# A hybrid encoder block: constants on another queue, and half of attention's q and k turned by VectorE instead of TensorE

## The chip, the cores and the metric

The kernel runs on one core of a Trainium2 chip. Its time is the device time of one execution in microseconds; lower is better. The engines are TensorE (PE; its weight loads are PEld), VectorE (DVE), ScalarE (ACT), GpSimd (POOL) and SyncE (SP). SyncE only issues DMAs here; GpSimd issues DMAs and clears a few buffers.

## The reference

One layer of a block over 512 tokens (8 rows x 64 columns) of width 1024, in float32:

```python
x = x + FFN_RES * _swiglu(_rmsnorm(x, norm_ffn1), w_ffn1_gu, w_ffn1_down)      # d_ff 2816, FFN_RES 0.5
h = _rmsnorm(x, norm_mix)
xr, gr, q, k, v, ga, gb = jnp.split(h @ w_in, splits, axis=-1)                 # 7 x 1024 columns
xc = _centred_dwconv(xr, conv_w, conv_b)                                       # width 4
h_fwd = _rglru_scan(xc, ...); h_bwd = reversed scan                            # gated linear recurrences
y_lru = (h_fwd + h_bwd) * jax.nn.gelu(gr)
q = _rmsnorm(q per head, q_norm) * HEAD_DIM ** -0.5                            # 16 heads of 64
k = _rmsnorm(k per head, k_norm)
y_att = _neighbourhood_attention(q, k, v, rel_pos_bias)                        # window 8 rows x 16 columns
y = jax.nn.sigmoid(ga) * y_lru + jax.nn.sigmoid(gb) * y_att
x = x + y @ w_out
x = x + FFN_RES * _swiglu(_rmsnorm(x, norm_ffn2), w_ffn2_gu, w_ffn2_down)
```

## The kernel before

**Precision.** Each large product is made of three fast matmuls. An operand is split into a high part (a cast to float32r, by ScalarE or VectorE) and a low part (the rest, by a VectorE subtraction), and TensorE adds high·high, low·high and high·low in PSUM (names `xh`, `xl` for activations, `wh`, `wl` for weights). `split` (line 136) makes both; `load_w` (line 153) loads 512 KB of weights and splits them, with three raw buffers and four of each part, so weights are cast two or three chunks ahead of their use.

**Order.** A scheduler places the instructions on each engine by what is ready and by priority, not strictly in the order of the program; `after` and `hold` (lines 239 and 245) tie an instruction behind another one, `hold` behind the matmul that was written last. Buffers come from pools by tag: `big` has 42 tiles of 128 x 512, `pair` four of 1024 columns, `PT` five, `pt` two. There are four PSUM tiles of a kind called `acc` and four called `aux`.

**First stage** (`ffn` with `lead`, lines 469 to 494). For each of eight tiles k of x, SyncE loads x and a weight tile (the first weight tile on ScalarE's queue), ScalarE casts xh, casts the weights, squares x and scales it, VectorE makes the low parts, and TensorE runs 12 matmuls: for each of four token blocks xh·wh, xl·wh, xh·wl. xh needs the norm's scale, a column of `small`, a table of 114 constants per partition that GpSimd's queue loads (line 725). Eight matmuls on a tile of ones run ahead of this (line 131). Then the first feed-forward layer goes on in `strassen` (line 291).

**Middle stages.** `xr` projection and convolution, the recurrences (`lru`, line 799), then for each half hf of the heads q, k and v (`qk_raw`, `v_get`), then the gate projections (`gates`, line 1162: 24 chunks of 24 matmuls), then the output projection and the second feed-forward layer. Side work lies in "lanes": generators that `weave` advances at given rates while the projections go on (rates per stage in `RATE`). Attention is the lane `att`; the rest of v's layout is `v`, the recurrences are `lru`.

**Attention of a half** (`heads`, line 986). q and k come as tokens x features (four tiles each, `raws`). They are scaled by the norm (line 999); then for each fi of four pairs of heads `start(fi)` turns a 128 x 128 block per token group with TensorE, four for q (line 1008) and four for k (line 1010), into two aux tiles, and splits them into qh, ql, kh, kl, with the norm's gain `gq8` or `gk` (lines 1014 to 1019). `scores` (line 1023) runs the score matmuls (line 1040), VectorE adds the bias table `bm` and takes the maximum (line 1060), ScalarE does the exponential (line 1067), VectorE divides by the sum (line 1072). `ship` turns p by 32 x 32 blocks on VectorE, writes it to DRAM on SyncE's queue and fetches it turned on GpSimd's (line 1088, tile `PT`); `apply` multiplies by v (line 1103), for the second half two units later. `bias(g)` asks for the next table after the scores. `hT<-hd` and `PT<-pd` already use this way of turning: VectorE by blocks, and a DMA round trip through DRAM for the order of the blocks.

Of the kernel before, what the change touches and what calls it, by code (L numbers as in the profile page):

```python
# [9 lines left out]
F32 = mybir.dt.float32  # L10
# [70 lines left out]
    "t1": {"att": 0.75, "tail": 0.75, "lru": 2},  # L81
    "g": {"att": 0.7, "tail": 0.7, "lru": 1.5, "v": 0.5},
# [4 lines left out]
def block_kernel(ctx: ExitStack, tc, a, out):  # L87
# [19 lines left out]
    NBIG = 42  # L107
# [72 lines left out]
    def make_xg(gcol, tag):  # L180
# [6 lines left out]
        def one(k):  # L187
            g = small[:, gcol + k : gcol + k + 1]
            x = xres[k]
            mark["xh"] = nc.scalar.activation(xh[k], x, AF.Copy, scale=g)  # L190
            return nc.vector.scalar_tensor_tensor(xl[k], x, g, xh[k].bitcast(F32), ALU.mult, ALU.subtract)
# [269 lines left out]
    def ffn(wgu, ws, wd, xh, xl, forms, ssum, plain, res, emit_out, lead=None, end=None):  # L461
# [7 lines left out]
        if lead is not None:  # L469
            pre = [aux_t() for _ in range(NCB)]  # L470
            for k in range(KT):
# [6 lines left out]
                if k == 0:  # L478
                    cast = nc.vector.tensor_copy(H, raw)
                    after(lead[1](k), cast)  # L480
# [5 lines left out]
                for tb in range(NCB):  # L486
                    s = slice(tb * P, (tb + 1) * P)
                    nc.tensor.matmul(pre[tb], xh[k][:, s], H, start=k == 0, stop=False)
                    nc.tensor.matmul(pre[tb], xl[k][:, s], H, start=False, stop=False)  # L489
                    mark["mm"] = nc.tensor.matmul(pre[tb], xh[k][:, s], L, start=False, stop=k == KT - 1)  # L490
# [165 lines left out]
    lanes = {"att": [], "tail": [], "lru": [], "v": []}  # L656
    due = {"att": 0.0, "tail": 0.0, "lru": 0.0, "v": 0.0}
# [113 lines left out]
    gk = small[:, C_KN : C_KN + 1]  # L771
# [27 lines left out]
    def lru():  # L799
# [128 lines left out]
    def qk_raw(w, hf, st):  # L928
# [6 lines left out]
        for j, t in enumerate(raws):  # L935
            sq = big_t(n="sq")
# [49 lines left out]
    def heads(hf, raws, st):  # L986
# [9 lines left out]
        for w in range(2):  # L996
            for j in range(NCB):
                t = raws[w][j].rearrange("p (h d) -> p h d", d=HD)
                hold(nc.vector.tensor_tensor(t, t, rq[:, w, j, :].unsqueeze(2).to_broadcast([P, 8, HD]), ALU.mult))
            yield  # L1000
        qk, rss, soft, PTs = {}, {}, {}, {}


        def start(fi):
            fs = slice(fi * P, (fi + 1) * P)
            pq, pk = aux_t(), aux_t()
            for j in range(NCB):
                hold(nc.tensor.transpose(pq[:, j * P : (j + 1) * P], raws[0][j][:, fs], ident))
            for j in range(NCB):
                hold(nc.tensor.transpose(perm(pk)[:, j], raws[1][j][:, fs], ident))  # L1010
            rev = lambda t: t.rearrange("p (j t) -> p j t", j=NCB)[:, :, ::-1]
            fwd = lambda t: t.rearrange("p (j t) -> p j t", j=NCB)
            qh, ql, kh, kl = (big_t(F32R, n=n) for n in ("qh", "ql", "kh", "kl"))
            nc.scalar.activation(rev(qh), fwd(pq), AF.Copy, scale=gq8)
            with tc.high_priority():
                nc.vector.scalar_tensor_tensor(rev(ql), fwd(pq), gq8, rev(qh.bitcast(F32)), ALU.mult, ALU.subtract)
            nc.scalar.activation(kh, pk, AF.Copy, scale=gk)
            with tc.high_priority():
                mark["kl"] = nc.vector.scalar_tensor_tensor(kl, pk, gk, kh.bitcast(F32), ALU.mult, ALU.subtract)
# [3 lines left out]
        def scores(fi, n2s):  # L1023
# [22 lines left out]
            for n2, hp in [(n2, hp) for n2 in n2s for hp in range(2)]:  # L1046
# [78 lines left out]
        for i, (fi, n2s) in enumerate(units):  # L1125
            behind = scores(fi, n2s)
# [4 lines left out]
            if 0 in n2s:  # L1131
                if fi < 3:
                    start(fi + 1)
                if hf * 4 + fi + 1 < KT:
                    bias(hf * 4 + fi + 1)
# [18 lines left out]
    for hf in range(2):  # L1154
        st = tiny.tile([P, 2, NCB, 8], F32, tag="st", name=nm("st"))
        raws = [qk_raw(0, hf, st), qk_raw(1, hf, st)]
        v_get(hf)
        lanes["att"].append(heads(hf, raws, st))
# [148 lines left out]
```

## Time and profile before

| | us |
|---|---|
| three runs | 1086.52, 1087.53 (median), 1088.55 |
| profiled execution | 1086.78 |
| its span | 1085.0 |
| TensorE busy / weight loads | 1077.1 / 884.3 |
| VectorE busy | 770.1 |
| ScalarE busy | 561.9 |
| GpSimd busy | 198.6 |

The profile is of one execution; the span is from its first to its last instruction. In its rows, a line such as L1008 is a line of the kernel, "out<-in" names the tiles written and read, "x4" counts instructions. A row of the timeline has start, duration, engine, line, operation, tiles and, in brackets, how long the engine had been idle and what ended that. A row of the chain has start, time and the work that held the chain there. A row of the waits has the total, the number and the longest. Matmul durations overlap in the timeline, so their pitch is read from the chain.

### The profile page before, as it was taken

How to read it: one execution, taken by the hardware profiler on the slowest of the kernel's cores; microseconds unless marked ns; L12 is line 12 of the kernel's file. 1: busy time of each engine (PE TensorE's matmuls, PEld its weight loads, DVE VectorE, ACT ScalarE, POOL GpSimd, SP SyncE). 2: the span in 40 equal slices, each digit the busy share in tenths (PEclk: the TensorE clock that was granted, in tenths of full speed). 3: DMA queues.
4: the chain of work that ended last, by engine and by line, in shares of the span. 5: the costliest groups of instructions: out<-in, count | busy, mean ns of one | idle time of the engine just before them, and what ended most of it. 6: DMA issues, size and time to landing. Idle time of an engine off the chain costs nothing.

```text
span 1085.0 us, 14411 instructions
## 1 busy us (share of the span) xinstructions
PE 1077.1 (99%) x5121; PEld 884.3 (82%) x5121; DVE 770.1 (71%) x1222; ACT 561.9 (52%) x866; POOL 198.6 (18%) x341
## 2 busy tenths in 40 slices
PE   8999999999999999999999999999999999999998
PEld 7888888888888778788877888888888888888887
DVE  7699788774327776999868987759677787764322
ACT  7755554553215768876444643446455555544320
POOL 0101012432000441331335232000000001342000
PEclk9999999999999999999999999999999999999999
DMA  8788765875324585573778586664476777676212
GB/s 334 187 232 212 217 164 148 230 250 179 99 81 140 175 239 154 166 218 101 226 234 223 169 237 205 192 233 161 95 193 182 190 206 166 177 252 194 94 73 78
DMA packets 67352, 198.18 MB, mean 183 GB/s; under 512 B 10944, under 2 KB 12736, under 8 KB 67280
## 3 DMA queue, kind: packets, MB, share of 16 engines
q1 hardware_dynamic: 46592, 136.60, 37.6%
q0 software_dynamic: 20544, 60.40, 25.1%
q8 instruction: 40, 0.66, 0.2%
q14 instruction: 32, 0.26, 0.1%
q10 hardware_dynamic: 144, 0.26, 0.1%
HBM read 162.06 MB, written 26.74 MB: 174 GB/s over the span
## 4 chain that ended last, share of the span: by engine, by line
PE 97%; DMA 1%; DVE 1%; ACT 0%; issue 0%; POOL 0%; ACTq 0%; POOLq 0%
PE acc L316 20%; PE aux L316 15%; PE acc L166 11%; PE acc L167 11%; PE acc L168 11%; PE acc L921 4%; PE acc L922 4%; PE acc L923 4%; PE aux L166 4%; PE aux L168 4%; PE aux L167 4%; PE aux L1103 1%; PE aux L832 1%; DMA vd<-v 1%; PE aux L1040 1%; PE aux L489 1%
## 5 line engine op out<-in xcount | busy, mean ns | idle before, releaser
L141 DVE TENSOR_TENSOR wl<-wraw,wh 128x1024 fp32r<-128x1024 f32 (+2 forms) x147 | 168.8, 1149 | 154.0 <-ACT wh L138 151.0
L138 ACT ACTIVATE wh<-wraw 128x1024 fp32r<-128x1024 f32 (+2 forms) x135 | 134.5, 998 | 225.9 <-PE acc L167 157.5
L141 DVE TENSOR_TENSOR wl<-pair,wh 128x1024 fp32r<-128x1024 f32 x80 | 97.4, 1220 | 44.5 <-ACT wh L138 44.3
L138 ACT ACTIVATE wh<-pair 128x1024 fp32r<-128x1024 f32 x80 | 84.7, 1061 | 75.8 <-PE aux L316 47.8
L166 PE MATMUL acc<-xh,wh 128*128 128x512 f32 x288 | 114.0, 396 | 0.0
L168 PE MATMUL acc<-xh,wl 128*128 128x512 f32 x288 | 112.5, 391 | 0.0
L167 PE MATMUL acc<-xl,wh 128*128 128x512 f32 x288 | 112.5, 391 | 0.0
L316 PE MATMUL aux<-wh,s 128*128 128x512 f32 x320 | 98.5, 389 | 0.0
L316 PE MATMUL acc<-wh,s 128*128 128x512 f32 x320 | 98.5, 389 | 0.0
L921 PE MATMUL acc<-wh,xh 128*128 128x512 f32 x192 | 75.7, 394 | 0.0
L922 PE MATMUL acc<-wh,xl 128*128 128x512 f32 x192 | 74.8, 389 | 0.0
L923 PE MATMUL acc<-wl,xh 128*128 128x512 f32 x192 | 74.7, 389 | 0.0
L316 PEld LDWEIGHTS aux<-wh,s 128*128 128x128 f32 x320 | 60.1, 188 | 12.5
L316 PEld LDWEIGHTS acc<-wh,s 128*128 128x128 f32 x320 | 60.0, 188 | 12.5
L167 PE MATMUL aux<-hl,wh 128*128 128x512 f32 (+1 forms) x179 | 69.3, 387 | 0.0
L168 PE MATMUL aux<-hh,wl 128*128 128x512 f32 (+1 forms) x179 | 69.3, 387 | 0.0
L166 PE MATMUL aux<-hh,wh 128*128 128x512 f32 (+1 forms) x179 | 69.0, 387 | 0.0
L168 PE MATMUL acc<-hh,wl 128*128 128x512 f32 (+1 forms) x176 | 68.1, 387 | 0.0
L167 PE MATMUL acc<-hl,wh 128*128 128x512 f32 (+1 forms) x176 | 68.1, 387 | 0.0
L166 PE MATMUL acc<-hh,wh 128*128 128x512 f32 (+1 forms) x176 | 68.0, 387 | 0.0
L166 PEld LDWEIGHTS acc<-xh,wh 128*128 128x128 f32 x288 | 54.1, 188 | 13.0 <-issue 2.3
L168 PEld LDWEIGHTS acc<-xh,wl 128*128 128x128 f32 x288 | 54.1, 188 | 11.6 <-issue 0.4
(231 smaller groups left out, 2416.7 us busy)
## 6 DMA issues: line engine op xcount, KB each, us to landing
wraw<-wqkv SPq DMA_DIRECT2D x24, 512.0 KB, 4.8
wraw<-wg SPq DMA_DIRECT2D x24, 512.0 KB, 8.3
wraw<-w1d SPq DMA_DIRECT2D x22, 512.0 KB, 4.1
wraw<-w2d SPq DMA_DIRECT2D x22, 512.0 KB, 3.5
PT<-w1s SPq DMA_DIRECT2D x20, 512.0 KB, 6.0
hT<-hd POOLq DMA_DIRECT2D x80, 128.0 KB, 4.2
PT<-w2s SPq DMA_DIRECT2D x20, 512.0 KB, 4.4
hd<-ht SPq DMA_DIRECT2D x32, 256.0 KB, 6.0
```

The costliest lines, as they stand in the source:

```text
L138: mark["H"] = nc.scalar.activation(H, raw, AF.Copy)
L141: mark["L"] = nc.vector.tensor_tensor(L, raw, H.bitcast(F32), ALU.subtract)
L166: nc.tensor.matmul(ps, wh, xh, start=first, stop=False, skip_group_check=skip)
L167: nc.tensor.matmul(ps, wh, xl, start=False, stop=False, skip_group_check=skip)
L168: mark["mm"] = nc.tensor.matmul(ps, wl, xh, start=False, stop=last, skip_group_check=skip)
L316: mark["mm"] = nc.tensor.matmul(pss[tb], x_[:, s], w_[:, c], start=first and k == 0 and x_ is xh_ and w_ is H, stop=k == 3 and w_ is L, sk ...
L489: nc.tensor.matmul(pre[tb], xl[k][:, s], H, start=False, stop=False)
L832: prev, mm = mm, nc.tensor.matmul(ps[d][b], W[w][o, c], X[x][o], start=x == 1, stop=w + x == 0)
L921: nc.tensor.matmul(pss[j], xh[kk][:, tj], H[:, s], start=kk == 0, stop=False)
L922: nc.tensor.matmul(pss[j], xl[kk][:, tj], H[:, s], start=False, stop=False)
L923: mark["mm"] = nc.tensor.matmul(pss[j], xh[kk][:, tj], L[:, s], start=False, stop=kk == KT - 1)
L1040: mm = hold(nc.tensor.matmul(ps[hp][:, cs], q_[o, n * P : (n + 1) * P], keys(k_[o]), start=k_ is kl, stop=q_ is ql))
```

## The change

- The constants `small` go on SyncE's queue, behind the first tile of x, instead of GpSimd's.
- In the first stage the cast of the first x tile is done in two halves of 256 columns. For k = 0 the matmuls run in another order: first xh·wh for the four token blocks, then xh·wl, then xl·wh.
- For the second half of the heads q and k are no longer turned by TensorE. A new lane `prep` (`norm_qk`), with its own rate of one step per weave, scales q and k of one token group, turns both by 32 x 32 blocks on VectorE into a `pair` tile and writes it to DRAM (`qd`, 512 KB, four times) on SyncE's queue. `fetch` reads one fi back in the right order with four DMAs on GpSimd's queue, in pieces of 256 bytes, into a single buffer `xqk`; the fetch of fi + 1 is asked for when `start(fi)` has used the buffer. `start` of the second half reads that tile instead of PSUM. The first half stays as it was.
- The gain of k is folded into the one of q (`gq8`), so kh is a plain cast and kl a plain subtraction.
- In the second half ScalarE divides p by the sum, not VectorE. All 24 weight casts of the gate projections go to ScalarE (12 were VectorE's).
- The next bias table is asked for ahead of the scores.
- Buffers: `big` has 40 tiles instead of 42; the squares of q and k use the two `pt` buffers; three tiles th of the recurrences use `xqk` and `PT`.

```diff
-    "t1": {"att": 0.75, "tail": 0.75, "lru": 2},
-    "g": {"att": 0.7, "tail": 0.7, "lru": 1.5, "v": 0.5},
+    "t1": {"att": 0.75, "tail": 0.75, "lru": 2, "prep": 1.0},
+    "g": {"att": 0.7, "tail": 0.7, "lru": 1.5, "v": 0.5, "prep": 1.0},
...
-    NBIG = 42
+    NBIG = 40
...
-        def one(k):
+        def one(k, parts=1):
             g = small[:, gcol + k : gcol + k + 1]
             x = xres[k]
-            mark["xh"] = nc.scalar.activation(xh[k], x, AF.Copy, scale=g)
+            for h in range(parts):
+                s = slice(h * T // parts, (h + 1) * T // parts)
+                mark["xh"] = nc.scalar.activation(xh[k][:, s], x[:, s], AF.Copy, scale=g)
...
-                    after(lead[1](k), cast)
+                    after(lead[1](k, 2), cast)
...
+                steps = [(tb, *p) for p in ((xh[k], H), (xl[k], H), (xh[k], L)) for tb in range(NCB)] if k == 0 else [
+                    (tb, *p) for tb in range(NCB) for p in ((xh[k], H), (xl[k], H), (xh[k], L))]
+                if k == 0:
+                    steps = steps[:4] + steps[8:] + steps[4:8]
...
-            tc.keep_in_program_order(nc.gpsimd.dma_start(small, a["small"]))
+            tc.keep_in_program_order(nc.sync.dma_start(small, a["small"]))
...
-    gk = small[:, C_KN : C_KN + 1]
+    nc.vector.tensor_tensor(gq8, gq8, small[:, C_KN : C_KN + 1], ALU.mult)
...
-            th = big_t(n="th")
+            if d == 1 and f < 3:
+                th = big.tile([P, T], F32, name=nm("th"), **(dict(tag="xqk", bufs=1) if f == 0 else dict(tag="PT", bufs=5)))
+            else:
+                th = big_t(n="th")
...
-            sq = big_t(n="sq")
+            sq = big.tile([P, T], F32, tag="pt", bufs=2, name=nm("sq"))
...
+            if qd is not None:
+                t2 = pair_t().rearrange("p a b -> p (a b)")
+                for w in range(2):
+                    nc.vector.transpose(
+                        t2.rearrange("p (c f w i) -> p w f c i", c=NCB, f=4, w=2)[:, w],
+                        raws[w][j].rearrange("p (f c i) -> p f c i", c=NCB, i=32))
+                while out:
+                    hold(nc.sync.dma_start(*out.pop()))
+                out.append((qd[j], t2))
+                yield
...
+    def fetch(qd, fi):
+        t = xs[fi] = big.tile([P, NCB * NCB, 2, 32], F32, tag="xqk", bufs=1, name=nm("xqk"))
+        for c in range(NCB):
+            hold(nc.gpsimd.dma_start(
+                t[c * 32 : (c + 1) * 32].rearrange("p g w i -> p g (w i)"),
+                qd.rearrange("j (a i) c f x -> c f i (j a) x", a=NCB)[c, fi]))
...
+        if hf == 1:
+            until("prep", lambda: False)
...
+            if hf == 0:
+                (the transposes as before)
+            else:
+                x = xs.pop(fi).rearrange("p (j a) w i -> p w j a i", j=NCB)
+                xq, xk = x[:, 0], x[:, 1].rearrange("p j a (r c) -> p j a r c", r=2)
...
+            if hf == 1 and fi < 3:
+                fetch(qd, fi + 1)
...
-                    nc.vector.tensor_scalar(pt, pt, rs[:, hp, n : n + 1], None, ALU.mult)
+                    if hf == 0:
+                        nc.vector.tensor_scalar(pt, pt, rs[:, hp, n : n + 1], None, ALU.mult)
+                    else:
+                        nc.scalar.activation(pt, pt, AF.Copy, scale=rs[:, hp, n : n + 1])
...
+            if 0 in n2s and hf * 4 + fi + 1 < KT:
+                bias(hf * 4 + fi + 1)
             behind = scores(fi, n2s)
...
-            feat_chunk(a["wg3"][w * KT + f], KT, xh, xl, ps, 0, KT, f % 2 == 0, RATE[phase[0]])
+            feat_chunk(a["wg3"][w * KT + f], KT, xh, xl, ps, 0, KT, True, RATE[phase[0]])
```

More of the change, by code (lines that the diff above doesn't have):

```diff
@@ L485, in ffn @@
                 lead[2](k)
[L486 to L490, printed above, removed]
+                steps = [(tb, *p) for p in ((xh[k], H), (xl[k], H), (xh[k], L)) for tb in range(NCB)] if k == 0 else [
+                    (tb, *p) for tb in range(NCB) for p in ((xh[k], H), (xl[k], H), (xh[k], L))]
+                if k == 0:
+                    steps = steps[:4] + steps[8:] + steps[4:8]
+                for tb, x_, w_ in steps:
+                    mark["mm"] = nc.tensor.matmul(
+                        pre[tb], x_[:, tb * P : (tb + 1) * P], w_, start=k == 0 and x_ is xh[k] and w_ is H,
+                        stop=k == KT - 1 and w_ is L)
             for ps in pre:
@@ L653, in ffn @@
         end(t1, o)
-    lanes = {"att": [], "tail": [], "lru": [], "v": []}
-    due = {"att": 0.0, "tail": 0.0, "lru": 0.0, "v": 0.0}
+    lanes = {"att": [], "tail": [], "lru": [], "v": [], "prep": []}
+    due = {"att": 0.0, "tail": 0.0, "lru": 0.0, "v": 0.0, "prep": 0.0}
     def weave(rate):
@@ L995, in heads @@
         yield
-        for w in range(2):
-            for j in range(NCB):
+        out = []
+        for j in range(NCB):
+            for w in range(2):
                 t = raws[w][j].rearrange("p (h d) -> p h d", d=HD)
                 hold(nc.vector.tensor_tensor(t, t, rq[:, w, j, :].unsqueeze(2).to_broadcast([P, 8, HD]), ALU.mult))
-            yield
+            if qd is not None:
+                t2 = pair_t().rearrange("p a b -> p (a b)")
+                for w in range(2):
+                    nc.vector.transpose(
[5 more added lines that the diff above has]
+                yield
+            elif j % 2 == 1:
+                yield
@@ new lines, in norm_qk, with heads @@
+        if qd is not None:
+            hold(nc.sync.dma_start(*out.pop()))
+            yield
+            fetch(qd, 0)
+    xs = {}
+    def fetch(qd, fi):
[4 more added lines that the diff above has]
+                qd.rearrange("j (a i) c f x -> c f i (j a) x", a=NCB)[c, fi]))
+    def heads(hf, raws, qd):
+        if hf == 1:
+            until("prep", lambda: False)
@@ new lines, in start @@
+            if hf == 0:
+                fs = slice(fi * P, (fi + 1) * P)
+                pq, pk = aux_t(), aux_t()
+                for j in range(NCB):
+                    hold(nc.tensor.transpose(pq[:, j * P : (j + 1) * P], raws[0][j][:, fs], ident))
+                for j in range(NCB):
+                    hold(nc.tensor.transpose(perm(pk)[:, j], raws[1][j][:, fs], ident))
+                xq, xk = pq.rearrange("p (j t) -> p j t", j=NCB), pk
+                q_of, k_of = rev, lambda t: t
+            else:
+                x = xs.pop(fi).rearrange("p (j a) w i -> p w j a i", j=NCB)
+                xq, xk = x[:, 0], x[:, 1].rearrange("p j a (r c) -> p j a r c", r=2)
+                q_of = lambda t: rev(t).rearrange("p j (a i) -> p j a i", i=32)
+                k_of = lambda t: t.rearrange("p (a r j c) -> p j a r c", a=NCB, r=2, j=NCB)
@@ L1018, in start @@
+            hold(nc.scalar.activation(k_of(kh), xk, AF.Copy))
             with tc.high_priority():
[L1019 removed]
+                mark["kl"] = nc.vector.tensor_tensor(k_of(kl), xk, k_of(kh.bitcast(F32)), ALU.subtract)
+            if hf == 1 and fi < 3:
+                fetch(qd, fi + 1)
             grid = lambda t: t.rearrange("p (r c) -> p r c", r=ROWS)
@@ L1156, in block_kernel @@
         raws = [qk_raw(0, hf, st), qk_raw(1, hf, st)]
+        if hf == 1:
+            qd = dram.tile([NCB, P, NCB, 4, 64], F32, name="qd")
+            lanes["prep"].append(norm_qk(raws, st, qd))
         v_get(hf)
-        lanes["att"].append(heads(hf, raws, st))
+        if hf == 0:
+            lanes["att"].append(norm_qk(raws, st, None))
+        lanes["att"].append(heads(hf, raws, qd if hf == 1 else None))
         phase[0] = "t1" if hf == 0 else "g"
```

16 lines of the change are left out of this document (3 added, 13 removed).

## The prediction

> **What bounds the kernel now.** I read the busy table first, then the chain of work that ended last, then the waits of TensorE.
>
> ```profile
> span 1085.0 us, 14411 instructions
> PE 1077.1 (99%) x5121; PEld 884.3 (82%) x5121; DVE 770.1 (71%) x1222; ACT 561.9 (52%) x866; POOL 198.6 (18%) x341
> PE 97%; DMA 1%; DVE 1%; ACT 0%; issue 0%; POOL 0%; ACTq 0%; POOLq 0%
> PE aux L1103 <- DVE ql L1016: 0.5, 1, 0.5
> ```
>
> TensorE is busy 99% of the span and carries 97% of the chain. Its matmuls wait for work four times only: at the opening, twice in the first stage (2.21 and 0.28, in the next fence) and the 0.5 shown. So only two things can shorten this kernel: fewer TensorE instructions, or an earlier and quicker first stage. Work taken off VectorE is worth nothing by itself, and work put on ScalarE costs nothing until it makes TensorE wait. The sum below is against the profiled execution, 1086.78 us (span 1085.0); the median of the three runs, 1087.53, is 0.75 above it, and their spread is 2 us. I take 0.2% (2.2 us) as what a measurement can tell from no change.
>
> **First part: the constants on SyncE's queue, the halved first cast, the new order of the first matmuls.** The timeline of the first 8 us, then the chain there, then busy time by stretch (columns: us, PE, weight loads, DVE, ACT, POOL, granted clock, DMA share, GB/s):
>
> ```profile
> 0.74 0.41 ACTq L474 DMA_DIRECT2D wraw<-w1gu  x1
> 1.06 3.78 PE L132 MATMUL aux<-ones 128*128 128x128 f32 x16 [1.06 <-DVE pol L757]
> 4.32 0.43 DVE L479 CAST wh<-wraw 128x512 fp32r<-128x512 f32 x1 [3.29 <-DMA wraw<-w1gu]
> 6.28 0.72 ACT L190 ACTIVATE xh<-pair,small 128x512 fp32r<-128x512 f32 x1 [3.61 <-DMA small<-small]
> 7.06 0.50 PE L488 MATMUL aux<-wh,xh 128*128 128x512 f32 x1 [2.21 <-ACT xh L190]
> 7.84 0.50 PE L489 MATMUL aux<-wh,xl 128*128 128x512 f32 x1 [0.28 <-DVE xl L191]
> 9.46 0.68 DVE L141 TENSOR_TENSOR wl<-wraw,wh 128x512 fp32r<-128x512 f32 x1
> ...
> 1.60 4.66 DMA small<-small
> 9.03 0.43 PE aux L490
> 12.02 0.43 PE aux L488
> 31.26 5.44 PE acc L316 x24
> ...
> 9.00:12.00 3.00, 3.00 (x9) 2.32 (x8) 2.69 (x5) 3.00 (x7) 0.00 (x0) 0.50 1.05 406
> L138 ACT ACTIVATE hh<-hT 128x256 fp32r<-128x256 f32 x80 | 26.7, 402 | 0.0
> ```
>
> The first real matmul starts at 7.06. It waits for xh, and xh waits for the constants, which GpSimd's queue delivers 4.66 us after issue. The stage ends at 31.26, where the first product begins.
>
> (a) Earlier start. The first weight tile, asked for at 0.74 on the otherwise empty ScalarE queue, is there at 4.32, 3.6 us after issue. The constants now go out on SyncE's queue behind the first x tile, about 1.2. With the 3.6 us they land at 4.8 (estimate); at best at 4.3, at worst 4.66 us after issue, 5.9. Half a cast is 0.40 by the 128x256 row, so the first matmul starts at 4.8 + 0.05 + 0.40 = 5.25 instead of 7.06: gain 1.8, bounds 0.7 to 2.2. The weight's cast ends at 4.75 and does not hold it.
>
> (b) No wait for xl. Today the second matmul starts 0.78 after the first; the pitch is 5.44/24 = 0.227. In the new order four xh·wh and four xh·wl come first. wl (0.68 on VectorE after the cast's end at 4.75) is ready near 5.45 and wanted at 6.16; xl, after both halves at 5.65 and 0.75 on VectorE (estimate: the difference of 7.84 and xh's end at 7.00, less the start-up), is ready near 6.4 and wanted at 7.07. Gain 0.55, bounds 0 and 0.55.
>
> (c) The slow stretch. From 9.03 to 12.44 eight matmuls of the chain (first and last shown) take 0.43 each, not the pitch of 0.23, at a granted clock of 0.50: 8 x 0.20 = 1.6 us lost. It follows 2.2 us of idle TensorE between the warm-up matmuls (end 4.84) and the first real one. After the change this gap is 0.4 us, so I count the whole 1.6; bounds 0 (the stretch comes anyway) and 1.6. [...]
>
> (d) Operands of k=1 fall behind. ScalarE starts xh at 6.28, and wl of k=1 is ready at 10.14, 3.86 later; from 4.8 that is 8.7, and TensorE, now quick, wants it at 5.25 + 14 x 0.227 = 8.4. New wait 0.35, bounds 0 and 1.0 (the x and weight tiles go out one issue later, behind the constants). Later steps I count at nothing: the lists of the two engines are as today, and TensorE waits for none of them.
>
> Sum of the first part: 1.8 + 0.55 + 1.6 - 0.35 = 3.6, bounds -0.3 and 4.35.
>
> **Second part: q and k of the second half turned by VectorE.** It removes 32 TensorE transposes (lines 1008 and 1010, fi 0 to 3). The chain, columns start and time; the percentages are of 584 to 597:
>
> ```profile
> by line: PE acc L166 26.1%; PE acc L168 22.9%; PE acc L167 22.9%; PE aux L1103 18.5%; PE aux L1010 6.3%; PE aux L1008 4.7%
> ...
> 559.59 0.42 PE acc L166
> 604.04 0.59 PE aux L1008 x4
> 604.63 0.44 PE aux L1010 x4
> 605.07 0.23 PE acc L166
> 631.70 0.94 PE aux L1040 x12
> ```
>
> The first eight cost 11.0% of 13 us = 1.43. Each later eight cost 0.59 + 0.44 = 1.03 (three times). But the projection matmul after transposes takes 0.23 and after scores 0.42: this switch, now hidden in the transposes, stays, so each of the three is worth 1.03 - 0.19 = 0.84. Gain 1.43 + 3 x 0.84 = 3.9, bounds 3.4 and 4.5 (no switch). It is all on the path, since TensorE never stands still there.
>
> What it adds: eight transposes and a norm moved earlier on VectorE, 4 writes of 512 KB on SyncE's queue, 16 fetches on GpSimd's, and on ScalarE 32 divisions of p and 12 weight casts taken from VectorE.
>
> ```profile
> L381 DVE STREAM_TRANSPOSE ht<-u 128x512 f32<-128x512 f32 x20 | 13.3, 690 | 0.0
> L999 DVE TENSOR_TENSOR qk<-qk,rq 128x512 f32<-128x512 f32 x16 | 10.0, 682 | 0.0
> L140 DVE CAST wh<-wraw 128x1024 fp32r<-128x1024 f32 x12 | 8.3, 694 | 8.2 <-PE acc L167 7.2 <-PE acc L922 1.0
> L138 ACT ACTIVATE wh<-wraw 128x1024 fp32r<-128x1024 f32 x120 | 127.1, 1059 | 224.1 <-PE acc L167 156.9 <-issue 28.2 <-PE acc L922 16.8
> 520.00:540.00 20.00, 20.00 (x114) 16.02 (x115) 17.45 (x50) 7.92 (x24) 7.47 (x14) 1.00 0.72 222
> 540.00:560.00 20.00, 19.50 (x134) 15.86 (x131) 15.93 (x45) 8.98 (x22) 3.53 (x7) 1.00 0.69 232
> 560.00:680.00 120.00, 120.00 (x774) 98.03 (x773) 95.06 (x247) 54.97 (x120) 43.23 (x72) 1.00 0.71 211
> 537.60 8.59 DMA vd<-v
> 547.50 0.76 DVE ql L1016
> ```
>
> VectorE: the prep lane runs in v's projection and the first gate chunks, some 522 to 550. It brings 8 x 0.69 + 8 x 0.68 = 11.0 us; VectorE has 40 - 33.4 = 6.6 us free in 520 to 560, and three casts (0.69) leave, so it is over by about 2.4 us there. That is the one place where TensorE already waits (0.5 us on ql at 547.5), at the end of a run of v's evictions, the 8.59 us write of v and an exp; the new writes of q and k share that queue with it. I take 1.5 us of new TensorE wait; bounds 5 (VectorE's excess 2.4 and as much again for the slower write) and -0.5 (the present wait goes). Later VectorE is lighter, by the divisions of p and nine casts. ScalarE: 32 x 0.40 (the 128x256 row) + 12 x 1.06 = 25.6 us more in 560 to 680, where it is idle 65: nothing. SyncE: four more issues, nothing but the above. Bias tables earlier, 40 buffers for 42, squares in two shared buffers, th in other buffers: TensorE waits for none of these today; 0, bounds -1 and +1.
>
> Sum: 3.6 + 3.9 - 1.5 = 6.0. 1086.78 - 6.0 = 1080.8 by the profiled execution, 1081.5 by the median; I forecast 1081.
>
> **Rivals.**
>
> Slower: the fetches come too late for the scores. One unit, from VectorE's and GpSimd's timelines, and the issue and landing of a DMA in 256-byte pieces (va, min/median/max):
>
> ```profile
> 609.91 0.71 DVE L1019 SCALAR_TENSOR_TENSOR kl<-aux,small,kh 128x512 fp32r<-128x512 f32 x1
> 619.57 4.39 POOL L1088 DMA_DIRECT2D PT<-pd  x8 [10.52 <-PE aux L1040]
> 395.01 1.11 POOL L982 DMA_DIRECT2D bm<-rpb  x2 [0.51 <-DMA gate<-pair]
> L970 POOL DMA_DIRECT2D va<-vd x16: 768/774/821, 476.4 to 595.4; - x16
> DMA to landing us min/median/max: 2.5/4.1/7.7
> ```
>
> There is one xqk buffer, so a fetch waits for kl of the unit before (610.6), issues four DMAs at 0.77 to 1.55 (twice the pieces of va) and lands 4.1 to 7.7 later: 617.8 to 624.5. q and k then need some 3 us, and the scores want them at 631.7: 4 to 11 us to spare. If GpSimd takes the fetch only behind the eight PT issues (end 623.96), it lands at 631 to 638 and the scores are 2.4 to 9 us late, for two units: 5 to 18 us, a time of 1086 to 1099, near 1092. It decides for slower once each of the two is over (6.0 + 2.2)/2 = 4.1 us late. Against it: GpSimd's order is not the program's, since bias tables were issued at 395, a hundred us ahead of any scores; and a fetch is ready 9 us before PT. For it: PT's issues wait long in that queue. [...]
>
> The edge at 548 grows to its bound: 3.5 us more than counted, 1084.5.
>
> [...]
>
> It does nothing measurable: the constants land as late as now (first part at its lower end) and the edge at 548 takes 4 us: 1086.8 + 0.3 - 3.9 + 4 = 1087.
>
> **Chances.** Forecast 0.55 (own range 1078 to 1083.5); slow stretch stays 0.14; edge at its bound 0.13; no effect 0.08; late fetches 0.10. The first three are faster by over 0.2% (under 1085.3): 0.82; same 0.09, with the mild end of the late fetches; slower 0.09. The range 1077.5 to 1086 holds the first three save the edges of each, about 0.8.
>
> **What would show it.** Right: the wait for the constants under 1 us, the first real matmul near 5.2 and the first product near 27.7; no 0.50 clock around 9 to 12; lines 1008 and 1010 at 32 instead of 64 in sum; TensorE waits around 540 to 560 under 2 us. Wrong: TensorE waits on qh, ql or kl ahead of the scores of the second half, a clock of 0.50 in the first 15 us, ScalarE standing behind a fetch while weights are uncast, or a first product later than 29.

## The result, and the profile after

| | us |
|---|---|
| kernel before, five runs | 1086.46 to 1088.55, median 1087.53 |
| kernel after, five runs | 1104.17 to 1106.91, median 1105.45 |
| ratio after / before | 1.0169, 95% interval 1.0154 to 1.0183 |
| span of the profiled execution, before / after | 1085.0 / 1105.1 |

The forecast was 1081 (1077.5 to 1086). The change made the kernel 18 us slower. "Tile 4" to "tile 7" below are the four fi of the second half.

First the busy times and the chain's shares, on the page of the kernel after:

```profile
span 1105.1 us, 14403 instructions
PE 1079.6 (98%) x5089; PEld 888.0 (80%) x5089; DVE 760.8 (69%) x1187; ACT 586.8 (53%) x911; POOL 208.2 (19%) x356
PE 88%; DVE 4%; DMA 3%; ACT 2%; issue 1%; POOL 1%; SPq 0%; POOLq 0%; ACTq 0%; DVEq 0%
```

TensorE's waits from the middle of the kernel on (total, times, longest):

```profile
PE aux L1087 <- DVE kl L1064: 20.5, 4, 7.5
```

TensorE has 32 instructions less, and its share of the chain fell from 97% to 88%. There is one new row of waits, 20.5 us, ahead of the four sets of scores. The opening, first from the chain:

```profile
1.20 3.17 DMA small<-small
5.02 22.06 PE aux L493 x96
27.07 5.44 PE acc L318 x24
```

The first real matmuls in TensorE's timeline:

```profile
5.02 1.20 PE L493 MATMUL aux<-wh,xh 128*128 128x512 f32 x4 [0.40 <-ACT xh L192]
```

The stretch that ran at half clock before (the third value from the right is the granted clock):

```profile
9.00:12.00 3.00, 3.00 (x15) 2.49 (x14) 2.36 (x5) 3.00 (x6) 0.00 (x0) 1.00 1.05 404
```

The constants land at 4.4, the first real matmul starts at 5.02 and the first product at 27.07, 4.19 us earlier than before. The stretch at half clock is gone. The kernel after keeps this lead until 582 us. From there on it loses more than the lead, in four waits. They stand in TensorE's timeline:

```profile
588.51 0.58 PE L1087 MATMUL aux<-kl,qh 64*128 64x256 f32 x2 [5.91 <-DVE kl L1064]
613.75 0.58 PE L1087 MATMUL aux<-kl,qh 64*128 64x256 f32 x2 [7.50 <-DVE kl L1064]
634.39 0.40 PE L1087 MATMUL aux<-kl,qh 64*128 64x256 f32 x2 [3.54 <-DVE kl L1064]
654.26 0.58 PE L1087 MATMUL aux<-kl,qh 64*128 64x256 f32 x2 [3.54 <-DVE kl L1064]
```

Busy time in stretches of 20 us there:

```profile
580.00:600.00 20.00, 14.10 (x90) 11.37 (x89) 5.59 (x8) 2.66 (x4) 14.28 (x21) 0.83 0.63 157
600.00:620.00 20.00, 12.49 (x63) 10.25 (x62) 14.89 (x48) 15.40 (x42) 5.20 (x10) 0.74 0.56 180
620.00:640.00 20.00, 16.46 (x129) 13.74 (x128) 12.07 (x34) 13.06 (x35) 10.85 (x19) 0.91 0.69 208
640.00:660.00 20.00, 16.46 (x103) 14.07 (x102) 11.23 (x33) 11.11 (x30) 5.02 (x10) 0.83 0.61 184
```

The waits add up to 20.5 us. Behind each one the clock is down as well: 0.83, 0.74, 0.91, 0.83, where it was 1.00 before. With the two gains of the forecast, -4.2 and -3.9, and the 20.5, the span should be 1097.4; it is 1105.1, and I put the other 7.7 us down to the lower clock (the last section looks at this again).

Why does kl come late? The timelines of ScalarE, VectorE and GpSimd around the first of the four:

```profile
582.47 1.06 ACT L138 ACTIVATE wh<-wraw 128x1024 fp32r<-128x1024 f32 x1 [2.00 <-issue]
583.43 0.71 ACT L1059 ACTIVATE qh<-xqk,gq 128x512 fp32r<-128x512 f32 x1
584.05 0.61 ACT L1062 ACTIVATE kh<-xqk 128x512 fp32r<-128x512 f32 x1
600.66 1.06 ACT L138 ACTIVATE wh<-wraw 128x1024 fp32r<-128x1024 f32 x1 [16.00 <-issue]
...
582.65 0.69 DVE L1223 TENSOR_TENSOR pair<-acc,rstd 128x512 f32<-128x512 f32 x1 [3.30 <-PE acc L168]
583.56 1.23 DVE L141 TENSOR_TENSOR wl<-wraw,wh 128x1024 fp32r<-128x1024 f32 x1 [0.22 <-ACT wh L138]
584.70 2.49 DVE L1237 TENSOR_TENSOR A<-pair,th 128x512 f32<-128x512 f32 x4
587.11 0.75 DVE L1061 SCALAR_TENSOR_TENSOR ql<-xqk,gq,qh 128x512 fp32r<-128x512 f32 x1
587.77 0.69 DVE L1064 TENSOR_TENSOR kl<-xqk,kh 128x512 fp32r<-128x512 f32 x1
...
580.18 0.55 POOL L1138 DMA_DIRECT2D PT<-pd  x1 [0.41 <-DMA xqk<-qd]
```

TensorE ends a gate chunk at 582.6 and wants the scores next. On ScalarE qh stands behind a weight cast (wh) that needs the weight buffer of just that chunk (the row names only "issue", but in the trace's semaphore records the wait ahead of this cast ends at 582.40 with a matmul of the chunk, PE acc L167, and the timeline names PE acc L167 ahead of the same cast for tiles 6 and 7); on VectorE ql and kl stand behind that chunk's eviction (pair), the weight's low part and four multiplications. So the casts begin only when TensorE has run out of work, and TensorE then waits for 5.9 us of work on the two engines. The last row shows that a transfer of the fetched tile (by its place in the queue the last of the four) had landed by 580.18, 3.25 us ahead of qh: for this tile the data are not what is late. The landings in the trace say the same of the others: the last piece of tiles 4 to 7 landed at 579.9, 595.3, 628.1 and 641.5, and TensorE reached the scores at 582.6, 606.3, 630.9 and 650.7. (For tile 6 that is 2.8 us ahead, no more than its casts take.) ScalarE stood idle for 2.00 us with qh next but one in its queue, and took it up at 583.43, behind the weight cast that began at 582.47. After the casts ScalarE idles for 16.0 us more, since its next weight cast needs the buffer of a chunk that comes behind the late scores.

From this came three theories. T1, my own rival: the fetch is late (its round trip, its one buffer, or GpSimd's queue). T2: the q and k casts have a bad place in the queues of ScalarE and VectorE. T3: the 25 us of casts and divisions given to ScalarE make the scores wait. A scheduler had written the order of each queue. Counted in that order, the last cast ahead of each of the four scores needs the matmul one or two places ahead of the scores. In the kernel before, the last transpose of a tile, from which its casts are made, stands 27, 81, 49 and 61 matmuls ahead of its scores (counted in the trace). The expectations below use this distance; they take 0.216 us a matmul, where the chain of the kernel before shows 0.227.

### The profile page after: what moved, and what is told of

It reads as the page before. It is cut to its first block, busy times and chain, and to the rows that moved or that the text cites. A ratio compares the mean times of both kernels' runs of the same rounds, so it can differ in the third digit from the quotient of the medians.

```text
span 1105.1 us, 14403 instructions
## 1 busy us (share of the span) xinstructions
PE 1079.6 (98%) x5089; PEld 888.0 (80%) x5089; DVE 760.8 (69%) x1187; ACT 586.8 (53%) x911; POOL 208.2 (19%) x356
## 4 chain that ended last, share of the span: by engine, by line
PE 88%; DVE 4%; DMA 3%; ACT 2%; issue 1%; POOL 1%; SPq 0%; POOLq 0%; ACTq 0%; DVEq 0%
PE acc L318 19%; PE aux L318 15%; PE acc L166 9%; PE acc L167 9%; PE acc L168 9%; PE acc L929 4%; PE acc L930 4%; PE acc L931 4%; PE aux L168 4%; PE aux L167 4%; PE aux L166 4%; PE aux L493 2%; DMA pd<-pt 1%; PE aux L837 1%; PE aux L1153 1%
## 5 line engine op out<-in xcount | busy, mean ns | idle before, releaser
L138 ACT ACTIVATE wh<-wraw 128x1024 fp32r<-128x1024 f32 (+2 forms) x147 | 147.4, 1004 | 268.7 <-PE acc L167 180.6
L167 PE MATMUL acc<-xl,wh 128*128 128x512 f32 x288 | 113.1, 393 | 0.0
L167 PE MATMUL aux<-hl,wh 128*128 128x512 f32 (+1 forms) x179 | 69.3, 387 | 0.0
L167 PE MATMUL acc<-hl,wh 128*128 128x512 f32 (+1 forms) x176 | 68.1, 387 | 0.0
```

Of the source, the lines that this page charges most:

```text
L138: mark["H"] = nc.scalar.activation(H, raw, AF.Copy)
L167: nc.tensor.matmul(ps, wh, xl, start=False, stop=False, skip_group_check=skip)
```

## The experiments

Waits of TensorE ahead of the scores, from each trace's timeline (others: waits after 560 us for P or for weights). The ratios are to the kernel before, with 95% intervals.

| kernel | median us | ratio | tile 4 | 5 | 6 | 7 | others |
|---|---|---|---|---|---|---|---|
| lead_only | 1083.39 | 0.9965 (0.9952 to 0.9977) | 0 | 0 | 0 | 0 | 0 |
| no_turning | 1083.12 | 0.9965 (0.9953 to 0.9977) | 0 | 0 | 0 | 0 | 0 |
| scalar_back | 1110.72 | 1.0216 (1.0201 to 1.0232) | 9.88 | 8.44 | 3.54 | 3.54 | 0 |
| fetch_on_sync | 1087.52 | 1.0008 (0.9999 to 1.0017) | 0 | 0 | 3.54 | 3.27 | 0 |
| two_buffers | 1099.05 | 1.0105 (1.0091 to 1.0119) | 5.90 | 7.50 | 0 | 0 | 1.69 |
| gpsimd_later | 1098.93 | 1.0103 (1.0088 to 1.0119) | 0.24 | 12.96 | 0 | 0 | 4.34 |
| order_only | 1091.66 | 1.0051 (1.0032 to 1.0071) | 0.47 | 1.92 | 7.87 | 0 | 0 |
| order_gpsimd | 1088.84 | 1.0008 (0.9997 to 1.0019) | 0.47 | 2.56 | 2.32 | 0 | 2.75 |
| sync_two_buffers | 1086.57 | 0.9989 (0.9980 to 0.9998) | 0 | 0 | 0 | 0 | 5.54 |
| sync_later_scalar_back | 1082.41 | 0.9944 (0.9927 to 0.9962) | 0 | 0 | 3.86 | 0 | 0 |
| sync_order | 1080.03 | 0.9933 (0.9919 to 0.9948) | 0 | 0 | 0.58 | 0 | 0.99 |
| sync_later | 1078.14 | 0.9915 (0.9902 to 0.9929) | 0 | 0 | 0 | 0 | 0 |

**The lead alone, on the kernel before.** Besides the halved cast and the new list of matmuls of the diff:

```diff
-            tc.keep_in_program_order(nc.gpsimd.dma_start(small, a["small"]))
+            tc.keep_in_program_order(nc.sync.dma_start(small, a["small"]))
```

> The kernel before with the lead's part of the change alone: constants on SyncE's queue, first activation cast in two halves, new order of the first sixteen matmuls. The second half's transposes stay on TensorE. The trace of the kernel after shows the first product 4.19 us earlier (27.07 against 31.26), and no other part of the change can act there. All theories: 1083.3 us (1082.5 to 1084.5), a gain of 4.2. A gain under 2 would say that the lead's gain is given back later in the kernel.

Measured 1083.39, a gain of 3.9. The lead does what the profile of the kernel after shows, and nothing gives it back.

**The turning undone, the rest kept.**

```diff
-        if hf == 1:
-            qd = dram.tile(...)
-            lanes["prep"].append(norm_qk(raws, st, qd))
+        lanes["att"].append(norm_qk(raws, st, None))    # and heads(hf, raws, None)
```

> The kernel after with the turning undone: the second half's q and k are transposed by TensorE again, and nothing is written out or fetched. Lead, weight casts on ScalarE, divisions of p on ScalarE and bias tables ahead of the scores stay. T1 (the fetch comes too late on the chip) and T2 (the q and k casts got a bad place in ScalarE's and VectorE's queues because of the fetch): no wait ahead of the scores of the second half, 1083.5 us (1082 to 1086), the lead's gain alone. T3 (ScalarE's added 25 us of casts and divisions is what makes the scores wait): the waits stay in part, 1090 to 1104.

Measured 1083.12, the same as the lead alone. So the loss belongs to the turning, and ScalarE's added work costs nothing by itself. T3 falls here. (The trace has one wait, at 545.4 us and so ahead of the table's range: 1.58 us behind a ql, at the edge that the prediction priced. The medians do not show it.)

**ScalarE's work put back on VectorE, the turning kept.**

```diff
-            feat_chunk(..., True, RATE[phase[0]])
+            feat_chunk(..., f % 2 == 0, RATE[phase[0]])
-                        nc.scalar.activation(pt, pt, AF.Copy, scale=rs[:, hp, n : n + 1])
+                        nc.vector.tensor_scalar(pt, pt, rs[:, hp, n : n + 1], None, ALU.mult)
```

> The kernel after with ScalarE's added work put back: every second gate weight cast and the second half's divisions of p on VectorE, as before. The turning and the fetch stay. In the order of its queues the operands of all four scores of the second half still stand behind work that needs the matmul one or two instructions ahead of the scores. T2: waits ahead of all four scores stay, 1101 to 1110 us. T1: the same, the fetch is untouched. T3: the 20.5 us of waits go for the most part, 1080 to 1088.

Measured 1110.72, a little beyond the upper end for T2. All four waits stay and the first two grow: VectorE, where ql and kl stand in line, has more to do between the chunk's eviction and them. T3 falls again.

**The fetch on SyncE, nothing else changed.**

```diff
-            hold(nc.gpsimd.dma_start(    # in fetch()
+            hold(nc.sync.dma_start(
```

> The kernel after with one word changed: the four fetches of each feature tile are issued by SyncE and not by GpSimd. One buffer and the same round trip through memory stay. In the order of the queues, the last cast for the scores of tiles 4 and 5 now needs only work 37 and 25 matmuls ahead of the scores (8 and 5 us at 0.216 us each), that for tiles 6 and 7 still the matmul right ahead of them. T2 (the place in the queues): the waits at tiles 4 and 5 go (13.4 of the 20.5 us), those at 6 and 7 stay at 3 to 4 us each, and about half of the 8 us of halved clock goes: 1088 us (1085 to 1093). T1 in its narrow form (the round trip and the one buffer are too slow for the scores): the waits at 5, 6 and 7 stay, 1098 to 1107. T3: nothing changes, 1105.

TensorE's waits in its timeline:

```profile
616.33 0.58 PE L1087 MATMUL aux<-kl,qh 64*128 64x256 f32 x2 [3.54 <-DVE kl L1064]
637.13 0.58 PE L1087 MATMUL aux<-kl,qh 64*128 64x256 f32 x2 [3.27 <-DVE kl L1064]
```

The distances told which two waits go and which two stay, and the time, 1087.52 where 1088 was expected. The ten runs lie between 1086.71 and 1089.98, and the trace is of the slowest. But one word changed more than one thing here: the scheduler wrote another order (in TensorE's list 12 matmuls of a gate chunk moved too), and on the chip the requests go out from another queue. The next runs take these apart.

**Two buffers, each fetch asked for a tile earlier, on GpSimd.**

```diff
-            fetch(qd, 0)
+            fetch(qd, 0); fetch(qd, 1)       # buffers: tag PT with 6 instead of PT 5 and xqk 1
-            if hf == 1 and fi < 3: fetch(qd, fi + 1)
+            if hf == 1 and fi < 2: fetch(qd, fi + 2)
```

> The kernel after with a second buffer for the fetched tiles (taken from a pool enlarged by the first one's place) and each fetch asked for one tile earlier, still by GpSimd. In the order of the queues the last cast for tiles 4 and 5 still needs the matmul right ahead of the scores; for tiles 6 and 7 work 33 and 25 matmuls ahead. T2: waits at 4 and 5 stay (13.4 us), those at 6 and 7 go (7.1 us) with about half of the halved clock: 1094 us (1090 to 1098). T1 in its narrow form: with a buffer free the waits at 5, 6 and 7 go (14.6 us) and only that at 4 stays: 1086 (1083 to 1089).

```profile
PE aux L1088 <- DVE kl L1065: 13.4, 2, 7.5
PE aux L1154 <- DMA PT<-pd: 1.7, 1, 1.7
```

The 13.4 us of T2 to the digit. Tile 5 had its data asked for a tile earlier and still waits 7.50. So the one buffer is not what holds it. The time, 1099.05, lies 1 us above T2's range; P for the last tiles now comes 1.7 us late as well.

**GpSimd, two buffers, scores later.** Two buffers as above, but the fetch for tile 5 is asked for in `start(0)`, and three more steps lie ahead of the scores.

```diff
         if hf == 1:
             yield
+            yield; yield; yield
```

> The fetch stays on GpSimd's queue, with two buffers and three more empty steps ahead of the second half's first scores. In the order of the queues the last cast for tiles 4, 6 and 7 needs work 25, 25 and 37 matmuls ahead of the scores, for tile 5 the matmul right ahead. T2: one wait, at tile 5, of 3.5 to 7.5 us, with 1 to 3 us of halved clock: 1079.4 + 4.5 to 10 = 1084 to 1089. If it is GpSimd's queue itself that is too slow for the scores, waits stay at three or four tiles: 1092 to 1105.

The place was right (one wait, at tile 5) and its size wrong: 12.96 us, so 1098.93 where 1084 to 1089 was expected; P for the last tiles came 4.34 us late besides. The time falls into the range of the other theory, a queue of GpSimd that is too slow, but the waits do not: it wanted three or four, and tile 5's data had landed by 602.9, ahead of its scores at 611.0. VectorE's timeline, accumulator reads left out, says why:

```profile
611.07 0.69 DVE L1228 TENSOR_TENSOR pair<-acc,rstd 128x512 f32<-128x512 f32 x1 [4.21 <-PE acc L168]
...
613.13 2.49 DVE L1242 TENSOR_TENSOR A<-pair,th 128x512 f32<-128x512 f32 x4
615.53 0.35 DVE L1109 CUSTOM_DVE_ANT_0 so<-aux,bm 128x192 f32<-128x192 f32 x1
...
623.15 0.69 DVE L1066 TENSOR_TENSOR kl<-xqk,kh 128x512 fp32r<-128x512 f32 x1 [0.35 <-ACT kh L1064]
```

Between the eviction that ends the chunk and kl stands the whole softmax of the tile before (from 615.53). The distance says whether a wait comes; how long it is follows from the work between.

**Nothing but the order.** The fetch stays on GpSimd with one buffer, and TensorE's instruction list is the same. (In the order that came of it one fetch request on GpSimd and one write of P on SyncE also stand a few places earlier.)

```diff
+        for n0, kq, kl in turns:                 # in load_w; a turn is noted in start()
+            if nld[0] - n0 >= 5:
+                after(mark["H"], kq)
+                after(mark["L"], kl)
...
+            for n0, kq, kl in turns:             # in gates, behind the eviction ev
+                if nld[0] - n0 >= 1:
+                    after(ev, kl)
```

> The kernel after, with nothing changed but the order in ScalarE's and VectorE's queues: a gate weight's cast may not stand ahead of the q and k casts that were recorded five or more weight loads earlier, and a gate's eviction may not stand ahead of a tile's last cast recorded before it. Fetch, GpSimd's queue, one buffer, ScalarE's casts and divisions, and TensorE's whole order of instructions stay as they are. The last cast for tiles 4, 5, 6 and 7 then needs work 25, 57, 57 and 57 matmuls ahead of the scores. T2 (the place in the queues): the 20.5 us of waits fall to at most 2 us (at tile 4, where the fetch lands at about 580 us and the scores are reached at 582.6), the clock stays up, and the time is 1079.4 + 0 to 3 = 1081 us (1079 to 1083). T1 (the fetch itself is late, by its round trip, its one buffer or GpSimd's queue): waits of 3 us and more stay at three or four tiles, 1095 to 1106.

Both theories missed. The order alone takes off 13.8 us (1105.45 to 1091.66), so T2 is a large part of the loss. But 10.3 us of waits remain, most of them at tile 6. The timelines of GpSimd and of ScalarE:

```profile
603.12 0.69 POOL L1036 DMA_DIRECT2D xqk<-qd  x1 [0.78 <-issue]
603.80 2.21 POOL L1145 DMA_DIRECT2D PT<-pd  x4
606.00 0.67 POOL L1036 DMA_DIRECT2D xqk<-qd  x1
613.57 2.22 POOL L1145 DMA_DIRECT2D PT<-pd  x4 [6.90 <-DMA pd<-pt]
615.78 1.30 POOL L1036 DMA_DIRECT2D xqk<-qd  x2
...
620.78 0.72 ACT L1064 ACTIVATE qh<-xqk,gq 128x512 fp32r<-128x512 f32 x1 [6.21 <-DMA xqk<-qd]
```

The four requests for tile 6 are strewn among those for P, which wait 6.90 us for the softmax; the last two go out at 615.78, and now ScalarE does stand at qh waiting for the fetch (6.21). This is T1, in its GpSimd part. The runs of this kernel spread over 8 us (1089.08 to 1097.12); the trace is of the quickest.

**The same, with the requests together.**

```diff
+            if hf == 1 and fi < 3:
+                start(fi + 1)
             for n2 in n2s:
                 ship(fi, n2)
-            if 0 in n2s:
+            if hf == 0 and 0 in n2s:
```

> The kernel with the order rule alone (GpSimd's fetch, one buffer), and besides, in the second half, a tile's q and k casts and the next fetch are recorded ahead of the shipping of the tile before. In GpSimd's queue the four fetch requests for tile 6 and those for tile 7 then stand together, ahead of the requests for P of tiles 4 and 5, which wait for the softmax; in the kernel with the order rule alone tile 6's were strewn among them and it waited 7.9 us. T2 widened to GpSimd's queue: the 7.9 us at tile 6 go, 0.5 and 1.9 us at tiles 4 and 5 stay: 1091.7 - 7.9 - 1 to 2 of slower clock = 1082 us (1080 to 1085). T1 in its narrow form (the round trip through memory and the one buffer are too slow on this queue): tile 6 still waits 3 us and more, 1086 to 1092.

Tile 6's wait shrank from 7.87 to 2.32 us, but 1082 did not come: 1088.84. Waits of 2.56 us (tile 5) and 2.75 us (P for the last tiles) stand beside it, and in GpSimd's timeline the fourth request for tile 6 was held for 5.68 us by something that the trace does not show:

```profile
603.89 2.00 POOL L1036 DMA_DIRECT2D xqk<-qd  x3 [0.82 <-issue]
611.57 0.66 POOL L1036 DMA_DIRECT2D xqk<-qd  x1 [5.68 <-issue]
```

On GpSimd's queue, then, the scores of tiles 5 and 6 still wait some 2 us with the requests together. (Two groups of products with v also moved in TensorE's list; the 2.75 us of wait may come from that. The trace is of one of the slower runs, 1089.82 in 1085.15 to 1090.40.)

**The fetch on SyncE with two buffers.** The edits of the kernel with two buffers, and besides:

```diff
-            hold(nc.gpsimd.dma_start(    # in fetch()
+            hold(nc.sync.dma_start(
```

> The fetch on SyncE with two buffers, scores where the kernel after has them. In the order of the queues the last cast for tiles 4, 5, 6 and 7 needs work 13, 57, 33 and 25 matmuls ahead of the scores (2.8, 12, 7 and 5.4 us). T2: at most a short wait at tile 4 (its queue needs 3.3 us of VectorE work after that matmul: 0 to 1 us), none at the others: 1079.5 to 1081. T1 and the one buffer as the cause would give the same here; GpSimd's slower issue as the cause too.

No wait at the scores, yet 1086.57. TensorE's waits:

```profile
PE acc L166 <- ACT wh L138: 3.9, 1, 3.9
PE acc L168 <- DVE wl L141: 1.7, 1, 1.7
```

SyncE's timeline:

```profile
593.68 11.16 SPq L1032 DMA_DIRECT2D xqk<-qd  x8
...
610.23 1.56 SPq L157 DMA_DIRECT2D wraw<-wg  x3
```

Eight fetch requests hold SyncE's queue for 11.16 us (a request held it for 0.53 by the median of the sixteen, where GpSimd's took 0.66 in the kernel after), and the gate weights behind them are asked for at 610.23. Yet this is not what TensorE waits for: by the trace's semaphore records the three loads landed at 616.8, 619.2 and 622.2, and TensorE wanted the first at 623.0 (626.85 less 3.87). ScalarE's timeline says what held the casts:

```profile
623.27 0.61 ACT L1063 ACTIVATE kh<-xqk 128x512 fp32r<-128x512 f32 x1
624.79 1.06 ACT L1228 ACTIVATE pair<-pair 128x1024 f32<-128x1024 f32 x1 [0.90 <-DVE pair L1224]
625.75 2.93 ACT L138 ACTIVATE wh<-wraw 128x1024 fp32r<-128x1024 f32 x3
```

The three casts stand behind tile 7's kh and behind an activation of `pair`, which waits for the eviction of the chunk that TensorE has just ended, and they follow it without a gap. It is the fault of T2 again, with weights in the place of q and k. Why the scheduler put them there is not shown; that it counted the weights as late behind the fetches would be a guess. (The next expectation still takes the fetch for the cause.)

**The order rule on SyncE.** The edits of the order-only kernel, and besides:

```diff
-            hold(nc.gpsimd.dma_start(    # in fetch()
+            hold(nc.sync.dma_start(
```

> The same order rule with the fetch on SyncE, one buffer, no added step. The last cast for tiles 4 to 7 needs work 37, 57, 57 and 49 matmuls ahead of the scores. T2: no wait at the scores, 1078.1 as in the kernel with the added step (1077 to 1080), unless a weight cast that now stands behind a fetch comes late for its chunk, as in the kernel with two buffers: up to 1086.

Measured 1080.03, with 0.58 us of wait at the scores. One buffer and the round trip through memory are fast enough, so T1 in its narrow form falls.

**The fetch on SyncE and one more step ahead of the scores.**

```diff
-            hold(nc.gpsimd.dma_start(    # in fetch()
+            hold(nc.sync.dma_start(
...
         if hf == 1:
             yield
+            yield
```

> The kernel after with the fetch on SyncE and one more empty step of the attention lane ahead of the second half's first scores, which moves them all about one gate chunk later. One buffer. In the order of the queues the last cast for the scores of tiles 4, 5, 6 and 7 needs work 61, 37, 17 and 25 matmuls ahead of the scores (13, 8, 3.7 and 5.4 us). T2 (the place in the queues): no wait over 1 us ahead of the scores, the clock stays at 1.00, and both gains are kept, 1087.5 - 4.2 - 3.9 = 1079.4 us (1078 to 1081.5). T1 in its narrow form (one buffer's round trip is too slow): waits at tiles 5 to 7 stay, 1085 to 1095.

Measured 1078.14, faster than both kernels: 9.5 us below the kernel before, 27.3 below the one after. Its span is 1075.5. The stretch in which the kernel after lost most:

```profile
580.00:600.00 20.00, 20.00 (x130) 16.35 (x128) 13.05 (x35) 16.32 (x35) 10.18 (x17) 1.00 1.01 268
```

TensorE is busy all of the time and the clock is 1.00; it waits for nothing after its opening. Both intended gains are there at once.

**The same with ScalarE's work put back on VectorE.**

```diff
-            feat_chunk(..., True, RATE[phase[0]])
+            feat_chunk(..., f % 2 == 0, RATE[phase[0]])
-                        nc.scalar.activation(pt, pt, AF.Copy, scale=rs[:, hp, n : n + 1])
+                        nc.vector.tensor_scalar(pt, pt, rs[:, hp, n : n + 1], None, ALU.mult)
```

> The kernel with the fetch on SyncE and the added step, with ScalarE's added work put back on VectorE (every second gate weight cast, the divisions of p). The last cast for tiles 4 to 7 needs work 37, 37, 13 and 25 matmuls ahead of the scores. T2: within 1.5 us of 1078.1 (a short wait at tile 6 at most). T3 in the reverse (ScalarE's added work is what makes room on VectorE, so it is needed): waits of 3 us and more come back, above 1083.

Median 1082.41, outside the 1.5 us of T2: tile 6, where the distance was 13 matmuls, waited 3.86 us. The four runs were 1078.7, 1082.3, 1082.6 and 1083.5 and the trace is of the last, so the wait may not be in all of them. With the waits at the other tiles gone in both, moving this work to ScalarE looks useful, as it clears VectorE ahead of kl; one wait in one trace is little to go by.

## Why the prediction was wrong, point by point

**Lead (a) to (d), 3.6 us: right.** Measured 4.2 in the trace and 3.9 by the medians. The constants landed at 4.4 (4.8 counted) and (d) did not show (by its own figures, 8.7 less 8.4, it would be 0.3, not 0.35). The half-clock stretch (c), which had a chance of 0.14 of staying, went: TensorE's gap ahead of the first real matmul is 0.40 us instead of 2.21, and the clock from 9 to 12 us is 1.00 in the kernel after, in the three order kernels (order_only, order_gpsimd, sync_order), and in sync_two_buffers, sync_later and gpsimd_later. That the shorter gap would do this was my estimate from one row of the kernel before. For that kernel there is one trace, so whether it always had this stretch is open; by the last section it hung on little (the clock fell there after a step with 1.86 us of idle time, and in the kernel after stayed up after one with 1.89).

**Transposes, 3.9 us: right in kind.** From the lead alone to the kernel with SyncE and one more step the time falls by 5.25 us, above my bounds of 3.4 to 4.5. When the same gate matmuls are lined up in the two traces, 0.7 us of this lies ahead of 583 us, where the turning cannot act, and 4.5 us in the stage of the scores. That is the upper bound, the one without the switch: the 0.19 that I held back for each later set did not show.

**The edge at 548, 1.5 us: wrong, too dear.** TensorE does not wait there at all in the kernel after. VectorE's excess of 2.4 us was absorbed. (Without the turning, TensorE waited 1.58 us there.)

**ScalarE's 25.6 us at nothing: right as far as it goes.** Without the turning it cost nothing (1083.12 against 1083.39).

**What failed: q and k at nothing, with "4 to 11 us to spare".** This is the step in the first rival: "q and k then need some 3 us, and the scores want them at 631.7". It has three faults.
- I took the 3 us of casting as starting when the data land. In the kernel after they started when the queue got there (tile 4's qh at 583.43, 3.25 us behind the landing). For tile 4 the data were in and the casts stood behind a weight cast, an eviction, a low part and four multiplications. All but the multiplications need the chunk that TensorE finishes just before the scores, and the multiplications stand behind those that do. In the profile before there was room between the two: kl was ready 3.6, 7.4, 5.3 and 8.6 us ahead of the scores of tiles 4 to 7. The kl that the prediction quotes ends at 610.62 and is tile 5's, whose scores came at 618.03 (those at 631.70 are tile 6's):

```profile
618.03 0.39 PE L1040 MATMUL aux<-kl,qh 64*128 64x256 f32 x2
```

That room came with the transposes: their place in TensorE's list set the casts ahead, and with the transposes put back (the turning undone) no score waits. I removed the transposes and kept their room in the sum.
- I took the scores to stay where they were. With the lead, without 32 transposes and with the preparation moved to its own lane they come earlier. The first of the half were reached at 582.6 (588.51 less 5.91); in the chain of the kernel before they stood 20 us later (what this earlier place alone cost is not shown):

```profile
602.37 0.94 PE aux L1040 x12
```

- The late fetch was given a chance of 0.10 and two tiles, 1086 to 1099. Its GpSimd mechanism exists (in the order-only kernel ScalarE stood at tile 6's qh for 6.21 us until the fetch landed), but it did not make the waits of the kernel after, where the data had landed each time, and all four tiles waited. I also gave no price to the clock: 8 to 10 us on top of the waits.

One listed sign was exactly what came: "TensorE waits on qh, ql or kl ahead of the scores of the second half".

**How the loss divides.** By medians: 13.8 us for the order on ScalarE and VectorE (after to order-only), then 11.6 for GpSimd's queue (order-only to the same on SyncE), and 1.9 between that and the best kernel. The first two steps have their share of the lowered clock (its mean in the profiled executions is 0.988 after, 0.997 in order_only, 1.000 in the same on SyncE), and in the second TensorE's list differs by the 12 matmuls that moved. Taken in the other order, the move to SyncE alone brings 17.9, since it changes the casts' places too; so the split between the two is not sharp. Why the scheduler wrote the bad order is only inferred: it changed when the fetch moved to SyncE, though the q and k casts were untouched, so the order seems to rest on when the scheduler takes the fetch to be done.

## What to carry to other kernels

Before a producer is moved off the critical engine, ask what its old place fixed: here TensorE's transposes stood 27 matmuls or more ahead of the scores and the casts came soon after them; without the transposes the casts sank behind work that waits for TensorE itself. For each operand of the critical engine, find the last instruction ahead of it in its queue and ask which matmul that one needs; if it is the one right ahead of the use, there was a wait each time in these runs (3.27 to 12.96 us), however idle the queue's engine. The same question goes to DMA queues: requests that wait for the softmax (6.90 us in the order-only kernel) should not stand ahead of those that feed the scores.

## What the runs showed of the hardware that I had not expected

The waits of the kernel after cost more than themselves: 20.5 us of waits and some 9 us more. Granted clock (the third value from the right) in stretches of 2 us behind the first wait of the kernel after:

```profile
588.00:590.00 2.00, 1.49 (x14) 1.49 (x16) 0.46 (x1) 0.00 (x0) 1.31 (x3) 0.50 0.41 83
...
596.00:598.00 2.00, 2.00 (x33) 1.83 (x34) 0.00 (x0) 0.00 (x0) 2.00 (x5) 1.00 0.30 63
```

The clock is at 0.50 when TensorE starts again, and stays there for 6.23 us more (to 594.74). In that time the gate matmuls start 0.43 us apart (592.39, 592.82, 593.24), behind it 0.23 (595.32, 595.55). TensorE's busy time at 0.50 behind the four waits is 6.22, 4.88, 3.41 and 5.33 us; half of the sum, about 10 us, is my estimate of what the lower clock took. The sum with the forecast's gains left 7.7 for it; with the measured ones it is 9.1, for the best kernel's trace, without waits and at full clock, has a span of 1075.5, and 1105.1 - 1075.5 - 20.5 = 9.1. The length of a wait alone did not decide this. In the kernel with the order rule and the requests together, the stretches just behind the wait of 2.56 us (tile 5) and that of 2.32 us (tile 6):

```profile
600.00:602.00 2.00, 1.24 (x20) 1.27 (x22) 2.00 (x4) 2.00 (x3) 2.00 (x4) 1.00 0.78 294
...
618.00:620.00 2.00, 1.95 (x26) 1.72 (x28) 2.00 (x3) 2.00 (x3) 1.55 (x3) 0.88 0.86 300
620.00:622.00 2.00, 2.00 (x17) 1.67 (x18) 2.00 (x6) 1.19 (x5) 0.75 (x2) 0.50 0.82 191
```

Behind the longer wait the clock is 1.00, behind the shorter one 0.50. The clock records of the traces, set against the idle time of TensorE (whose matmul ends are modelled), say more. In the kernel after the clock falls at 587.91, 608.39, 635.70 and 652.76 us: 20.48, 27.31 and 17.07 apart, which is 6, 8 and 5 times 3.413. The rises, at 594.74, 618.63, 639.11 and 659.59, lie on the same grid. In the kernel before the half-clock stretch goes from 8.90 to 12.31, one step of that length, and its grid has another place: a step ends at 5.49 and at 8.90, in the kernel after at 4.24 and at 7.65. Between the opening and the end of these two kernels the clock changes nowhere else. In the kernel after it fell after steps of the grid in which TensorE had idled 3.41, 2.15, 2.11 and 2.04 us, and stayed up after steps with 1.89 and 1.43. In the kernel before it fell after a step with 1.86. In the kernel with the requests together the mean clock of 0.88 from 618 to 620 puts the fall at about 619.5; of the wait of 2.32 us some 1.94 then lay in one step, while the wait of 2.56 lay across two, with some 0.84 and 1.72. What decides between 1.86 and 1.89 is not shown.

The fetch itself was quicker than forecast. From the view of its tile in the kernel after (ns min/median/max, then landing):

```profile
L1031 POOL DMA_DIRECT2D xqk<-qd x16: 651/661/694, 565.1 to 638.8; - x16
DMA to landing us min/median/max: 2.5/3.6/6.7
```

A request of 128 KB in 256-byte pieces held GpSimd for 0.66 us and landed after 3.6 (median), where I had counted 0.77 to 1.55 and 4.1 to 7.7. In the kernel after the transfer was not what the scores waited for.
